# Hybrid attention block: gate projections of the 'b' heads turned token-major, transposes issued in pairs, key copies by DMA

## The chip, the cores and the metric

One core of a Trainium2 chip runs the whole layer. The metric is the device time of one execution in microseconds. Before the change it is 446.06 us, the median of three runs (445.18 to 448.8).

The engines are named as the profile names them: PE is TensorE (matmul), PEld its weight loads, DVE VectorE, ACT ScalarE, POOL GpSimd, SP SyncE, which here issues DMAs. A q behind a name (SPq) is that engine's instruction queue.

## The reference

```
h = x @ w_in                                  # x: 1024 tokens x 1024
q_a, k_a, v_a, z_a, q_b, k_b, v_b, z_b = split(h)
y_a = neighborhood_attention(q_a, k_a, v_a, rel_bias)      # 8 heads, 8x16 window on a 16x64 grid
y_b = windowed_gqa_with_sink(rotary(q_b), rotary(k_b), v_b, sink)   # 8 query heads, 2 key heads, |i-j| <= 128
mixed = concat(y_a * silu(z_a), y_b * silu(z_b))
y = mixed @ w_out
out = layer_norm(2**0.25 * x + y)
```

All products keep fp32-like precision: operands are split into a high and a low fp16 part, and high*high, high*low and low*high are added up.

## The kernel before

**Projections.** w_in is cut into 21 groups of 128 output columns, worked off in the list ORDER: q0 to q3, k0 to k3 and z0 to z3 for the 'a' heads, qb0 to qb3, kb and zb0 to zb3 for the 'b' heads (z is a gate; each group has two heads of 64). `project` (L358) does one group in two halves of 512 tokens, 24 matmuls of 512 columns for each half: the weight part is the stationary operand, x the moving one, and the result has the group's columns on the partitions and the tokens along the row. The weights' low and high parts are made by `w_split` (L191): ACT writes the high part (L199), POOL scales the raw weights and subtracts (L204, L205). The first six groups (NPRO) are done one after the other; the other 15 are filled in between the attention's matmuls, so many at each step (`pump_to`, FILL_AT).

**The attention.** 128 units: first 64 of the 'b' heads (group p, head j of the pair, block of 128 queries), then 64 of the 'a' heads. The main loop (L1181) has a step for each unit: `stage_qk` makes the scores in a PSUM bank (L816, L817; four banks) and DVE adds bias and takes the maximum (L826); `stage_exp` has ACT take the exponent (L842); one step later `stage_tr` splits the probabilities into high and low fp16 parts (ACT L852, DVE L853) and turns them by a DMA transpose from SP (L856). Four units are a quad. `stage_pv` multiplies the four units' turned probabilities with the values (L881, 33 or 36 matmuls of 64 columns), 9 steps after the quad's first unit; a step later `stage_on` divides by the sums (DVE L887, L890), giving `on` with the tokens on the partitions; after the quad of the pair's second head, `stage_ot` turns `on` by four PE transposes (L901), and DVE multiplies the result into the gate z (L904 for 'b', L910 for 'a').

**Queries and keys.** A block of a qb group is turned by rotary positions: ACT copies it from PSUM (L311), DVE shuffles it (L312), POOL multiplies by cos and sin and adds (L313 to L315). ACT then writes the high part for each of the two heads (L259) and POOL the low part (L265); the score matmul of the units that use them waits for that. For the keys, both parts are copied to the other 64 partitions by POOL (L295).

**The order of the work.** What is not written at its place goes through a recording layer: `enq` puts an operation in one of four queues (act, dve, pool, sp) with the operations it needs and a priority, and at fixed points of each step `pop` records the first one or two whose needs were recorded in an earlier step (for SP's results, two more steps later: `lag`). NP is the number that POOL gets at each step. `need` records an operation at once, with all that it needs, where a stage can't be recorded without it. What is recorded runs in that order on its engine.

**Output projection.** `m_queue` (L1009) splits the gated products m of the 'b' heads from step M_AT on: ACT high part (L1013), POOL low part (L1014). `out_mms` (L1021) multiplies 128 tokens of m with w_out; its first products fill the last steps, the rest follows after the attention (`final`), with the normalisation on DVE, ACT and POOL.

**Buffers.** z of each group has a tile of 1024 fp32; some share it with tables: the cos table has the slot "zc", which the gate zb3 gets later.

Of the kernel before, what the change touches and what calls it, by code (L numbers as in the profile page):

```python
# [15 lines left out]
S = 1024  # L16
# [20 lines left out]
ZTAG = {"z3": "zv", "zb3": "zc", "z2": "zs", "zb1": "zd", "zb2": "ze"}  # L37
# [9 lines left out]
WO_SCALE = 55  # L47
M_AT = [105, 112, 118, 120]
# [13 lines left out]
def hybrid_block(ctx, tc, xT, x, wt, wv, wo, bias, sink, gain, lbias, cos, sin, bmask, out):  # L62
# [220 lines left out]
    def split_k(p, half, src, dep=None):  # L283
# [3 lines left out]
        eng = "pool" if dep and clock["step"] is not None else "dve"  # L287
        for j in range(2):
            a, o = slice(64 * j, 64 * j + 64), slice(64 - 64 * j, 128 - 64 * j)
            hi, lo = split_hl(lambda j=j, a=a: own("kh", p, j)[a, sl], lambda j=j, a=a: own("kl", p, j)[a, sl],  # L290
                              src[a], dep is None, eng)

            def dup_(w, j=j, a=a, o=o):
                t = own(w, p, j)
                nc.gpsimd.tensor_copy(t[o, sl], t[a, sl])  # L295
# [4 lines left out]
            dup = [enq("pool", lambda d=dup_: d("kh"), o1, after=32 if dep else 0),  # L300
                   enq("pool", lambda d=dup_: d("kl"), o2, after=36 if dep else 0)]
            stk_ops.setdefault((p, j, half), []).extend(dup)
# [44 lines left out]
    def z_col(e):  # L347
        i = 0 if e in (4, 0, 5) else 1 if e == 1 else 2
# [8 lines left out]

    def project(name):  # L358
        n = ORDER.index(name)
# [397 lines left out]
    split = [ap.tile([128, 3, 2, 128], F16, name=f"split{i}", bufs=1) for i in range(NSPLIT)]  # L757
# [87 lines left out]
    def stage_tr(u):  # L845
        g, p, j, t, _ = u
        n, ch = geom(u)
        pt = st.pop((u, "p"))
        c, m = ch[0], len(ch)
        hl = split[units.index(u) % NSPLIT]  # L850
        src = pt[:, :n].rearrange("p (k c) -> p k c", c=c)
        nc.scalar.activation(hl[:, :m, 0, :c], src, AF.Copy, scale=PSCALE)  # L852
        nc.vector.scalar_tensor_tensor(hl[:, :m, 1, :c], src, PSCALE, hl[:, :m, 0, :c],  # L853
                                       op0=ALU.mult, op1=ALU.subtract)
        tr = ap.tile([128, 6, 128], F16, tag="tr", name="tr", bufs=BH)
        nc.sync.dma_start(tr[:, :2 * m, :], hl[:, :m].rearrange("p k i c -> p (k i c)"), transpose=True)  # L856
        st[u, "tr"] = tr
# [24 lines left out]

    def stage_on(q):
# [4 lines left out]
        if j == 0:  # L888
            on[g, p, h] = ap.tile([128, 4, 2, HD], F32, tag="on", name="on", bufs=2)
        nc.vector.tensor_mul(on[g, p, h][:, :, j, :], ps[:, :4 * HD].rearrange("p (m e) -> p m e", e=HD),  # L890
                             ri.unsqueeze(2).to_broadcast([128, 4, HD]))

    def stage_ot(q):
        g, p, j, h = quad(q)
        if j == 0:
            return
        need(*stk_ops.get(f"zb{p}" if g == "b" else f"z{p}", ()))
# [4 lines left out]
        if g == "b":  # L902
            z = zt[4 + p][:, 512 * h:512 * h + 512]
            nc.vector.scalar_tensor_tensor(z, ps, z_col(4 + p), z, op0=ALU.mult, op1=ALU.mult)  # L904
        else:
            for i in range(2):
                b = 2 * h + i
                z = zt[p].rearrange("p (r c) -> p r c", c=GW)[:, :, 16 * b:16 * b + 16]
                src = ps[:, 256 * i:256 * i + 256].rearrange("p (r c) -> p r c", c=16)
                nc.vector.scalar_tensor_tensor(z, src, z_col(p), z, op0=ALU.mult, op1=ALU.mult)  # L910
# [19 lines left out]
    def m_alloc(e):  # L930
        if e >= 4:
            t = big_tile(f"m{e}", (128, 2, S), F16)
        else:
            t = tiles["fp"].tile([128, 2, S], F16, tag="m", name=f"m{e}", bufs=4)
        mh[e], ml[e] = t[:, 0, :], t[:, 1, :]

    def m_split(e, sl, hi, lo):
        hi(mh[e][:, sl], zt[e][:, sl])
        lo(ml[e][:, sl], zt[e][:, sl], mh[e][:, sl])  # L939
# [69 lines left out]
    def m_queue(e):  # L1009
        m_alloc(e)  # L1010
        m_ops[e] = []
        for h in (slice(0, 512), slice(512, S)):
            o = enq("act", lambda h=h: nc.scalar.copy(mh[e][:, h], zt[e][:, h]))  # L1013
            m_ops[e].append(enq("pool", lambda h=h: nc.gpsimd.tensor_sub(  # L1014
                ml[e][:, h], zt[e][:, h], mh[e][:, h]), o))
# [5 lines left out]
    def out_mms(t, a, ps, es, c=(0, 512)):  # L1021
        o, w = c
        ts, cs = slice(128 * t, 128 * t + 128), slice(o, o + w)
        ps = ps[:, o:o + w]
        for e in es:
# [4 lines left out]
            for i, (lh, rh) in enumerate(((mh[e], woh), (mh[e], wol), (ml[e], woh))):  # L1030
                nc.tensor.matmul(ps, lh[:, ts], rh[:, cs],  # L1031
# [16 lines left out]
    def final():  # L1048
# [7 lines left out]
        for e in EO[4:]:  # L1056
            m_split(e, slice(0, 512), nc.scalar.copy, nc.vector.tensor_sub)
            for n in (WO_SEQ.index((e, 0)), WO_SEQ.index((e, 1))):
                wo_split(n)
        for e in EO[4:]:  # L1060
            m_split(e, slice(512, S), nc.scalar.copy, nc.vector.tensor_sub)
        gb, bb = gain_tile[0], zslot("bb")
# [113 lines left out]
    def gain_load():  # L1176
        gain_tile.append(zslot("gb"))
# [3 lines left out]
    for i in range(-LD, NU + LO):  # L1181
# [25 lines left out]
        if i == 131:  # L1207
            enq("sp", gain_load, *m_ops[4])
# [32 lines left out]
        pop("dve", ND if i < M_AT[1] else 2, same=True)  # L1241
        if i < NU:
            stage_exp(units[i])
        pop("act", NA if i < M_AT[0] and len(queues["act"]) < 5 else 2)
# [80 lines left out]
```

## Time and profile before

| what | us |
|---|---|
| median of 3 runs | 446.06 |
| the profiled execution | 446.49 |
| its span, first to last instruction | 444.7 |
| PE busy | 437.5 |
| DVE busy | 344.2 |
| ACT busy | 308.3 |
| POOL busy | 221.6 |

The TensorE clock was granted at 0.995 of full speed over the span. A page of the profile groups instructions: line, engine, operation, tile written and tiles read (out<-in), sizes (partitions x elements), how many; then the busy time, the mean time of one in ns, the idle time of the engine just before them and what ended most of it. A timeline has the start in us from the span's beginning, the length, the engine, the line and the operation; equal neighbours are merged (x2), and in square brackets stands the idle time before it and what ended it. The chain of waits is the work that ended last, followed back from the last instruction.

### The profile page before, as it was taken

What the parts mean: (1) busy time and instruction counts of PE and PEld (TensorE: products, weight loads), DVE (VectorE), ACT (ScalarE), POOL (GpSimd) and SP (SyncE); (2) the same over time, 40 slices, a digit from 0 to 9 for tenths busy, and PEclk for the clock granted to TensorE, in tenths of its full rate; (3) what the DMA queues carried; (4) which work ended last, traced back from release to release, by engine and by line L of the source; (5) the groups of instructions that cost most, each with busy time, mean ns of one, the idle gap of its engine ahead of it and who ended that gap; (6) DMA issues with size and microseconds to landing.
All of it is one profiled execution on the core that took longest, in us unless ns stands there. A gap on an engine that the chain in (4) does not pass through costs nothing.

```text
span 444.7 us, 9505 instructions
## 1 busy us (share of the span) xinstructions
PE 437.5 (98%) x3289; PEld 255.5 (57%) x3289; DVE 344.2 (77%) x849; ACT 308.3 (69%) x700; POOL 221.6 (50%) x235
## 2 busy tenths in 40 slices
PE   9999999999999999999999999999999999999994
PEld 8997754444445565655565655656555654444453
DVE  5978967438986898887988888888878837589944
ACT  5759789766499988887868887888778946302401
POOL 0110074646839558866506767765574405205740
PEclk9999999999999999999999999999999999999997
DMA  8921469984659999587978899998999998103612
GB/s 272 390 91 60 145 235 339 336 292 169 213 127 214 206 190 181 98 162 143 164 127 175 169 182 180 213 170 213 192 204 253 167 172 347 55 0 102 232 69 72
DMA packets 133841, 81.39 MB, mean 183 GB/s; under 512 B 101280, under 2 KB 113440, under 8 KB 133536
## 3 DMA queue, kind: packets, MB, share of 16 engines
q1 hardware_dynamic: 133648, 80.64, 75.4%
q8 instruction: 26, 0.43, 0.4%
q14 instruction: 23, 0.19, 0.2%
q10 hardware_dynamic: 144, 0.13, 0.1%
HBM read 50.34 MB, written 9.96 MB: 136 GB/s over the span
## 4 chain that ended last, share of the span: by engine, by line
PE 91%; DMA 3%; POOL 3%; DVE 1%; issue 1%; ACT 1%; SPq 0%; POOLq 0%; DVEq 0%; ACTq 0%
PE ps_pj L379 44%; PE ps_s L1031 9%; PE ps_s L486 6%; PE ps_t L881 6%; PE ps_pj L1031 5%; PE ps_t L1031 5%; PE ps_s L816 4%; PE ps_s L817 4%; PE ps_pj L486 3%; PE ps_t L486 3%; DMA bias<-in_bias 3%; PE ps_t L901 1%; POOL wl L205 1%; PE ps_t L412 1%; POOL ks L295 1%
## 5 line engine op out<-in xcount | busy, mean ns | idle before, releaser
L379 PE MATMUL ps_pj<-xf,wh 128*128 128x512 f16 x672 | 202.1, 379 | 0.1
L379 PE MATMUL ps_pj<-xf,wl 128*128 128x512 f16 x336 | 127.3, 379 | 0.0
L379 PEld LDWEIGHTS <-wh 128*128 128x128 f16 x672 | 63.7, 98 | 60.4 <-DVE ks L263 0.5
L842 ACT ACTIVATE ps_s<-sn,nm 128x385 f32<-128x385 f32 (+3 forms) x128 | 70.1, 548 | 25.1 <-DVE nm L826 24.6
L853 DVE SCALAR_TENSOR_TENSOR split<-ps_s,split 128x384 f16<-128x384 f32 (+2 forms) x128 | 65.7, 513 | 27.5 <-ACT split L852 25.9
L1031 PEld LDWEIGHTS <-m 128*128 128x128 f16 x432 | 40.0, 98 | 41.1 <-DVE m L939 0.2
L852 ACT ACTIVATE split<-ps_s 128x384 f16<-128x384 f32 (+2 forms) x128 | 57.8, 452 | 2.5 <-DMA tr<-split 0.2
L204 POOL TENSOR_SCALAR wr<-wr,wsc 128x512 f32<-128x512 f32 x26 | 20.6, 791 | 68.1 <-ACT wh L199 61.6
L379 PEld LDWEIGHTS <-wl 128*128 128x128 f16 x336 | 32.9, 98 | 37.4
L826 DVE CUSTOM_DVE_ANT_0 sn<-ps_s,bm,nsk 128x384 f32<-128x384 f32 (+1 forms) x64 | 40.7, 636 | 2.0 <-PE ps_s L817 1.7
L1031 PE MATMUL ps_s<-wo,m 128*128 128x512 f16 (+1 forms) x192 | 40.8, 366 | 0.0
L816 PE MATMUL ps_s<-ks,qs 128*128 128x384 f16 (+4 forms) x128 | 39.2, 306 | 0.3 <-DVE qs L263 0.3
L817 PE MATMUL ps_s<-ks,qs 128*128 128x384 f16 (+4 forms) x128 | 39.2, 306 | 0.0
L826 DVE CUSTOM_DVE_ANT_0 sn<-ps_s,bias,sg 128x264 f32<-128x264 f32 (+1 forms) x64 | 35.0, 547 | 4.5 <-issue 1.5
L881 PEld LDWEIGHTS <-tr 128*128 128x128 f16 (+1 forms) x1104 | 36.6, 98 | 2.2
L205 POOL TENSOR_TENSOR wl<-wr,wh 128x512 f16<-128x512 f32 x26 | 32.7, 1257 | 2.2
L788 POOL TENSOR_SCALAR bias<-bias,rsg 128x552 f32<-128x552 f32 (+1 forms) x24 | 19.1, 797 | 23.8 <-DMA bias<-in_bias 22.6
L295 POOL COPY ks<-ks 64x512 f16<-64x512 f16 x40 | 26.0, 661 | 7.1 <-DVE ks L263 2.8
L1086 ACT ACTIVATE sd<-mv,eps 128x1 f32<-128x1 f32 x8 | 2.4, 295 | 36.5 <-DVE mv L1084 35.2
L1031 PE MATMUL ps_pj<-wo,m 128*128 128x512 f16 (+1 forms) x144 | 26.2, 326 | 0.0
L1130 POOL TENSOR_TENSOR xr<-xr,gb 128x512 f32<-128x512 f32 x7 | 9.8, 1396 | 32.4 <-ACT xr L1127 32.4
L842 ACT ACTIVATION_READ_ACCUMULATOR ps_s<-sn,nm 128x1 f32 x128 | 24.4, 190 | 0.0
(188 smaller groups left out, 813.8 us busy)
## 6 DMA issues: line engine op xcount, KB each, us to landing
ws<-in_wt SPq DMA_DIRECT2D x15, 512.0 KB, 5.9
wr<-in_wt SPq DMA_DIRECT2D x26, 256.0 KB, 3.6
wor<-in_wo SPq DMA_DIRECT2D x22, 256.0 KB, 3.5
bias<-in_bias SPq DMA_DIRECT2D x16, 276.0 KB, 3.3
xr<-in_x SPq DMA_DIRECT2D x8, 512.0 KB, 9.6
out<-xr SPq DMA_DIRECT2D x15, 256.0 KB, 2.1
bias<-in_bias SPq DMA_DIRECT2D x8, 368.0 KB, 3.8
wvraw<-in_wv SPq DMA_DIRECT2D x9, 320.0 KB, 5.8
```

The lines of the kernel that those rows point to most:

```text
L205: nc.gpsimd.tensor_sub(l, raw, h)
L295: nc.gpsimd.tensor_copy(t[o, sl], t[a, sl])
L379: nc.tensor.matmul(ps, a[:, k % 4, :], mv, start=(k == 0 and i == 0), stop=(k == KT - 1 and i == 2))
L486: nc.tensor.matmul(ps[:, :320], lh[:, ts], rh[:, cs], start=(k == ko[0] and i == 0), stop=(k == ko[-1] and i == 2))
L816: nc.tensor.matmul(ps[:, :m], q, sl[0], start=True, stop=False)
L817: nc.tensor.matmul(ps[:, :m], q, sl[1], start=False, stop=True)
L826: nc.vector.tensor_tensor_reduce(sn[:, :m], ps[:, :m], bias_t, sg[:, c:c + 1], init, op0=ALU.add, op1=ALU.min, accum_out=nm)
L842: nc.scalar.activation(pt[:, :m], sn[:, :m], AF.Exp, bias=nm, scale=-1.0, accum_out=sm[:, k:k + 1])
L852: nc.scalar.activation(hl[:, :m, 0, :c], src, AF.Copy, scale=PSCALE)
L853: nc.vector.scalar_tensor_tensor(hl[:, :m, 1, :c], src, PSCALE, hl[:, :m, 0, :c], op0=ALU.mult, op1=ALU.subtract)
L881: nc.tensor.matmul(ps[:, HD * m:HD * m + HD], a, b_, start=(i == 0), stop=(i == len(mms) - 1))
L1031: nc.tensor.matmul(ps, lh[:, ts], rh[:, cs], start=(e == EO[0] and i == 0), stop=(e == EO[-1] and i == 2))
```

## The change

- The gate projections zb0 to zb3 are done token-major (`project_rows`): 128 tokens of x are the stationary operand, the weights the moving one, in 96 matmuls of 128 columns for each half; z then has the tokens on the partitions. All four come in the first six groups.
- `stage_on` of the 'b' heads multiplies by the gate's scale too, and POOL multiplies `on` into z. The four PE transposes and DVE's product of `stage_ot` are left out for the 'b' heads.
- As m of the 'b' heads now has the tokens on the partitions, `m_queue` puts its two fp16 parts side by side and turns them by two DMA transposes for each group, which write over z's tile. It runs from steps 26, 42, 57 and 80 instead of 105, 112, 118 and 120.
- The probabilities of two units share a buffer (3 buffers of two instead of 6 of one; 4 of two instead of 9 of one for the turned ones), and one DMA transpose turns both after the second.
- In the main loop the keys are copied to the other 64 partitions by DMA from SP instead of by POOL.
- An operation that needs a result of POOL is recorded one step later (`lag` 1 for pool).
- SP may record two operations at each step instead of one before step 118. z1 gets the slot of the cos table. The rows of gain and bias are loaded into other buffers. The scale of w_out is made at step 60 instead of 55.

```
-LTT, LPP, BP, BH, BR, ND, NA, NX, F1 = 1, 6, 2, 9, 5, 1, 1, 6, 0.2
-NSPLIT, NP = 6, 2
-ORDER = ["zb0", "z0", "zb1", "kb", "qb0", "z1", "qb1", "zb2", "qb2", "k0", "qb3", "zb3", "q0", "k1", "q1",
+LTT, LPP, BP, BH, BR, ND, NA, NX, F1 = 1, 6, 2, 4, 5, 1, 1, 6, 0.2
+NSPLIT, NP = 3, 2
+ORDER = ["zb0", "zb1", "zb2", "kb", "qb0", "zb3", "qb1", "z0", "qb2", "k0", "qb3", "z1", "q0", "k1", "q1",
          "k2", "q2", "z2", "k3", "q3", "z3"]
-ZTAG = {"z3": "zv", "zb3": "zc", "z2": "zs", "zb1": "zd", "zb2": "ze"}
+ZTAG = {"z3": "zv", "z1": "zc", "z2": "zs", "zb2": "zd", "z0": "ze"}
-WO_SCALE = 55
-M_AT = [105, 112, 118, 120]
+WO_SCALE = 60
+M_AT = [26, 42, 57, 80]
+POP2_AT = (105, 112)
...
-            self.prio, self.born, self.lag = prio, clock["step"], 2 if eng == "sp" else 0
+            self.prio, self.born, self.lag = prio, clock["step"], {"sp": 2, "pool": 1}.get(eng, 0)
...
             def dup_(w, j=j, a=a, o=o):
                 t = own(w, p, j)
-                nc.gpsimd.tensor_copy(t[o, sl], t[a, sl])
+                if live:
+                    nc.sync.dma_start(t[o, sl], t[a, sl])
+                else:
+                    nc.gpsimd.tensor_copy(t[o, sl], t[a, sl])
...
+    def project_rows(name):
...
+        for half in range(2):
+            ps = new_group()
+            need(w_ops[2 * n], w_ops[2 * n + 1])
+            for c in range(96):
+                t, k, i = c // 24, c // 3 % 8, c % 3
...
+                ts = slice(128 * t, 128 * t + 128)
+                h, l = parts[2 * n + k // 4]
+                a, b = ((x16h, h), (x16l, h), (x16h, l))[i]
+                nc.tensor.matmul(ps[:, ts], a[half, k][:, ts], b[:, k % 4, :], start=(c % 24 == 0), stop=(c % 24 == 23))
+                if c % 4 == 3 and c < 95:
+                    yield
+            groups.append(evac(name, half, ps))
+            yield
...
     def stage_tr(u):
...
+        o = 0 if i % 2 == first else 3
+        hl = split[i // 2 % NSPLIT]
...
-        tr = ap.tile([128, 6, 128], F16, tag="tr", name="tr", bufs=BH)
-        nc.sync.dma_start(tr[:, :2 * m, :], hl[:, :m].rearrange("p k i c -> p (k i c)"), transpose=True)
-        st[u, "tr"] = tr
+        if i % 2 == 0:
+            return
+        tr = ap.tile([128, 12, 128], F16, tag="tr", name="tr", bufs=BH)
+        w = 2 * (len(sizes[0][1]) + len(sizes[1][1]))
+        nc.sync.dma_start(tr[:, :w, :], hl.rearrange("p k i c -> p (k i c)")[:, :128 * w], transpose=True)
...
     def stage_on(q):
...
+        if g == "a":
+            nc.vector.tensor_mul(o, src, rb)
+            return
+        nc.vector.scalar_tensor_tensor(o, src, z_col(4 + p), rb, op0=ALU.mult, op1=ALU.mult)
+        z = zt[4 + p].rearrange("p (t j e) -> p t j e", j=2, e=HD)[:, 4 * h:4 * h + 4, j, :]
+        gate_ops.setdefault(4 + p, []).append(enq("pool", lambda: nc.gpsimd.tensor_mul(z, z, o), prio=0.6))
 
     def stage_ot(q):
         g, p, j, h = quad(q)
-        if j == 0:
+        if j == 0 or g == "b":
             return
...
     def m_queue(e):
...
+            o = enq("act", lambda hr=hr, z=z: nc.scalar.copy(hr[:, :, 0, :], z), *gate_ops[e])
+            o = enq("pool", lambda hr=hr, z=z: nc.gpsimd.tensor_sub(hr[:, :, 1, :], z, hr[:, :, 0, :]), o)
+            m_ops[e].append(enq("sp", lambda hr=hr, out16=out16: nc.sync.dma_start(
+                out16, hr.rearrange("p t i f -> p (t i f)"), transpose=True), o))
...
         if bulk["last"] != i or (queues["sp"] and i - queues["sp"][0].born > 2):
-            pop("sp", 1 if i < 118 else 3)
+            pop("sp", 2 if i < 118 else 3)
```

More of the change, by code (lines that the diff above doesn't have):

```diff
@@ L287, in split_k @@
         eng = "pool" if dep and clock["step"] is not None else "dve"
+        live = clock["step"] is not None
+        to = "sp" if live else "pool"
         for j in range(2):
@@ L756, in hybrid_block @@
     units = unit_list()
-    split = [ap.tile([128, 3, 2, 128], F16, name=f"split{i}", bufs=1) for i in range(NSPLIT)]
+    split = [ap.tile([128, 6, 2, 128], F16, name=f"split{i}", bufs=1) for i in range(NSPLIT)]
     sns = [ap.tile([128, 388], F32, name=f"sn{i}", bufs=1) for i in range(2)]
@@ L1056, in final @@
         for e in EO[4:]:
[L1057 removed]
+            m_split(e, slice(0, 4), nc.scalar.copy, nc.vector.tensor_sub)
             for n in (WO_SEQ.index((e, 0)), WO_SEQ.index((e, 1))):
```

89 lines of the change are left out of this document (53 added, 36 removed).

## The prediction

> **What bounds the kernel now.** I read the page first, then the chain of waits in order of time, then the timelines of single engines. The page gives the span, the busy time of TensorE (PE), and the shares of the chain that ended last:
>
> ```profile
> span 444.7 us, 9505 instructions
> ...
> PE 437.5 (98%) x3289; PEld 255.5 (57%) x3289; DVE 344.2 (77%) x849; ACT 308.3 (69%) x700; POOL 221.6 (50%) x235
> ...
> PE 91%; DMA 3%; POOL 3%; DVE 1%; issue 1%; ACT 1%; SPq 0%; POOLq 0%; DVEq 0%; ACTq 0%
> ```
>
> A busy PE need not be PE at its peak, so the pitch of its matmuls has to be seen. The chain (start, length, what) gives it, since there each matmul follows the one before:
>
> ```profile
> 68.72 10.38 PE ps_pj L379 x48
> ...
> 149.89 0.96 PE ps_t L881 x33
> ...
> 434.25 2.69 PE ps_pj L1031 x48
> ```
>
> So 48 matmuls of 512 columns take 10.38 us, 216 ns each; 64 columns take 29 ns, with a new 128x128 weight tile for each; 128 columns take 56 ns, again with new weights each. Hardly a gap stands between them: of the score matmuls of L816, which wait for the q and k copies, the groups by line show 0.3 us of idle time.
>
> ```profile
> L816 PE MATMUL ps_s<-ks,qs 128*128 128x384 f16 (+4 forms) x128 | 39.2, 306 | 0.3 <-DVE qs L263 0.3
> ```
>
> PE is fed without a break from the first projection to the last output product. What changes the time is therefore matmul time added or removed, and any wait that reaches PE. The profiled execution took 446.49 us for its span of 444.7, 1.8 us lie around the span, and it stands 0.4 above the median of 446.06. The sum is made against 446.49.
>
> **PE's own work.** The gate projections of the 'b' heads (zb0 to zb3) become token-major: each of 8 halves has 96 matmuls of 128 columns in place of 24 of 512. That is 768 x 56 = 43.0 us instead of 192 x 216 = 41.5, or +1.5. The transposes of L901 go for the 'b' heads, 32 of 64. Their price is the distance from four of them to the next matmul, in the PE timeline:
>
> ```profile
> 157.17 0.60 PE L901 MATMUL ps_t<-identf,on 128*128 128x128 f32 x4
> 157.61 1.13 PE L881 MATMUL ps_t<-vb,tr 128*128 128x64 f16 x33
> ```
>
> 0.44 us for four, so 8 x 0.44 = 3.5 us go. PE's work falls by 2.0 us. The first projection now wants both weight halves within 14 matmuls (0.8 us) where it wanted the second after 12 of 216 ns; GpSimd's (POOL's) second low part ended at 60.43, and PE began at 59.37:
>
> ```profile
> 59.27 1.16 POOL L205 TENSOR_TENSOR wl<-wr,wh 128x512 f16<-128x512 f32 x1
> ```
>
> 60.43 less 59.37 + 0.8 is 0.3 us late: +0.3.
>
> **What is put on GpSimd in the 'b' stretch.** Sixteen gate products of 128x256 (nearest row L1099, 0.73 us) = 11.7 us; six of the eight subtractions for the output's low parts (L1014's kind, 1.16 us) move there = 7.0 us; of the key copies that become DMAs only 8 lie here (0.66 us each) = -5.3.
>
> ```profile
> L1099 POOL TENSOR_TENSOR xr<-xr,gb 128x256 f32<-128x256 f32 x1 | 0.7, 728 | 0.2 <-DVE stats L1080 0.2
> ```
>
> ```profile
> L1014 POOL TENSOR_TENSOR m<-z,m 128x512 f16<-128x512 f32 x8 | 9.1, 1161 | 3.8 <-ACT m L1013 3.8
> L295 POOL COPY ks<-ks 64x512 f16<-64x512 f16 x40 | 26.0, 661 | 7.1 <-DVE ks L263 2.8 <-ACT ks L257 1.5 <-DMA wr<-in_wt 0.6
> ```
>
> The load alone would be carried. The place is what counts. GpSimd works in order, and two things of the change set its order: results of GpSimd are used a step later, which moves the last step of each 'b' query block (the subtraction of L265, for which the score matmul waits) back; and each gate product waits for VectorE's `on`, made at L890, with everything behind it in the queue waiting too. I followed the recording layer's rules through the built program. The first subtraction of a block was recorded at steps 26, 31, 42 and 48 for use at steps 32, 36, 48 and 52; it is now recorded at 30, 36, 44 and 51. The one at 36 is drawn out only by the score matmul that needs it. Ahead of it in GpSimd's queue stand the gates recorded at steps 30, 34 and 50. (Step n is the n-th score matmul, from 0.) The score matmuls of steps 30, 32, 34, 36, 50 and 52 in the PE timeline:
>
> ```profile
> 174.97 0.33 PE L816 MATMUL ps_s<-ks,qs 128*128 128x384 f16 x1
> ...
> 178.11 0.27 PE L816 MATMUL ps_s<-ks,qs 128*128 128x256 f16 x1
> ...
> 182.20 0.33 PE L816 MATMUL ps_s<-ks,qs 128*128 128x384 f16 x1
> ...
> 185.44 0.33 PE L816 MATMUL ps_s<-ks,qs 128*128 128x384 f16 x1
> ...
> 212.42 0.33 PE L816 MATMUL ps_s<-ks,qs 128*128 128x384 f16 x1
> ...
> 215.66 0.33 PE L816 MATMUL ps_s<-ks,qs 128*128 128x384 f16 x1
> ```
>
> VectorE's `on` of steps 30, 34, 42 and 50, and (last) of step 110, whose score matmul stands below it:
>
> ```profile
> 177.39 0.42 DVE L890 TENSOR_TENSOR on<-ps_t,ri 128x256 f32<-128x256 f32 x1
> 184.87 0.42 DVE L890 TENSOR_TENSOR on<-ps_t,ri 128x256 f32<-128x256 f32 x1
> 199.55 0.42 DVE L890 TENSOR_TENSOR on<-ps_t,ri 128x256 f32<-128x256 f32 x1
> 215.91 0.42 DVE L890 TENSOR_TENSOR on<-ps_t,ri 128x256 f32<-128x256 f32 x1
> ...
> 328.66 0.42 DVE L890 TENSOR_TENSOR on<-ps_t,ri 128x256 f32<-128x256 f32 x1
> ```
>
> ```profile
> 327.05 0.28 PE L816 MATMUL ps_s<-ks,qs 128*128 128x264 f16 x1
> ```
>
> So `on` ends 2.8, 3.1 and 3.9 us after the score matmul of its step at 30, 34 and 50, and 2.0 us where VectorE keeps up best. It was nothing's business, since the next use was PE's transposes three steps on. Now GpSimd's queue hangs on it. Its rows:
>
> ```profile
> 163.00 1.27 POOL L313 TENSOR_TENSOR rp_raw<-rp_raw,cos 128x512 f32<-128x512 f32 x1 [3.07 <-DVE rp_sw L312]
> ...
> 169.72 2.38 POOL L265 TENSOR_TENSOR qs<-rp_raw,qs 64x512 f16<-64x512 f32 x2
> ...
> 173.44 0.69 POOL L204 TENSOR_SCALAR wr<-wr,wsc 128x512 f32<-128x512 f32 x1
> 174.22 1.16 POOL L205 TENSOR_TENSOR wl<-wr,wh 128x512 f16<-128x512 f32 x1
> ...
> 179.14 1.15 POOL L265 TENSOR_TENSOR qs<-rp_raw,qs 64x512 f16<-64x512 f32 x1
> ...
> 204.57 1.27 POOL L313 TENSOR_TENSOR rp_raw<-rp_raw,cos 128x512 f32<-128x512 f32 x1
> ...
> 211.16 1.16 POOL L265 TENSOR_TENSOR qs<-rp_raw,qs 64x512 f16<-64x512 f32 x1 [2.75 <-ACT qs L259]
> ```
>
> Before, the subtractions ended 7.2, 5.2 and 3.3 us ahead of steps 32, 36 and 52 (178.11 - 170.88, 185.44 - 180.29, 215.66 - 212.32). Now, counted from the score matmul at the gate's step, with 0.08 us between dependent GpSimd instructions (173.44 + 0.69 to 174.22) and 0.05 for the gated `on`, a scalar_tensor_tensor (477 ns, L910) where a multiply took 424:
>
> ```profile
> L910 DVE SCALAR_TENSOR_TENSOR z<-ps_t,zc,z 128x256 f32<-128x256 f32 x16 | 7.0, 477 | 7.8 <-PE ps_t L901 7.8
> ```
>
> A, step 32: `on` 2.89, gate 0.81, subtraction 1.23: ready at 4.9, due at 178.11 - 174.97 = 3.1. Late by 1.8 (1.0 with the best `on`). The queue itself says the same: from 163.00 and one step of 1.6 later, two rope products 2.5, two weight splits 3.7, two gates 1.5, rope sum, product, product 3.8, two output subtractions 2.3, one query subtraction 1.2: 15.0 us, ending at 179.6 for 178.1.
>
> B, step 36: `on` 3.14, gate 0.81, a weight split 2.0 that stands between, subtraction 1.23: 7.2, due at 3.24. Late by 3.9; 2.9 if VectorE has caught up while PE stood at A. I take 3.2.
>
> C, steps 45 to 48: ScalarE (ACT) writes z1 over the cos table and so waits for GpSimd's last cos product. It did so before, for 1.75 us, with no loss on PE:
>
> ```profile
> 205.87 0.69 ACT L341 ACTIVATE z<-ps_pj,invt 128x512 f32<-128x512 f32 x1 [1.75 <-POOL rp_raw L313]
> ```
>
> Now ahead of that product stand a gate that waits for `on` at 199.97, two output subtractions, a split and two query subtractions: 199.97 + 0.8 + 2.3 + 2.0 + 1.2 + 1.2 + 1.3 = 208.8, 2.9 later than 204.57 + 1.27. The four score banks cover some of that; between 0 and 2.9 I take 1.0.
>
> D, step 52: `on` 3.96, gate 0.81, subtraction 1.23: 6.0, due at 3.24. Late by 2.8; 0.8 with the best `on`; I take 2.2.
>
> A to D: 8.2 us, from 4.7 to 11.4.
>
> **Transposes in pairs.** A DMA goes out after the second unit of a pair, with up to 12 blocks instead of 6.
>
> ```profile
> L856 SPq DMA_TRANSPOSE tr<-split x128: 1188/1212/2615, 126.1 to 361.3; - x128
> ...
> DMA to landing us min/median/max: 2.5/3.4/6.2
> ```
>
> The sync queue (SP) is freed of 64 issues of 1.2 us and gets 8 for the output parts and 32 key copies; it was not PE's bound, so no gain. The last unit of a quad has no time to give: its transpose went out with the pair of issues at 139.14, plus 3.4 is 142.5, and PE took it at 142.93.
>
> ```profile
> 139.14 2.50 SPq L856 DMA_TRANSPOSE tr<-split  x2
> ```
>
> ```profile
> 142.93 1.12 PE L881 MATMUL ps_t<-vb,tr 128*128 128x64 f16 x33
> ```
>
> A pair's landing is not in the trace: between 3.4 (size costs nothing) and 6.8 (all doubles). Issues hardly vary with size, so I stay near the low end: half a microsecond, felt by a few of 32 quads, +2.0 (0 to 16). The key copies are wanted at least 7 steps after they can start and cost nothing; uncovered, each would cost a landing of some 3 us. On SP a key copy waits for the ACT or VectorE part that it copies, with transposes behind it; these parts are recorded a step earlier, so I cost it at nothing. The buffers hold 6 units of split as before and 8 of tr; a buffer of split comes free one step later, 1.6 us of a cover of 6 steps less a landing. The output's parts are made some 40 steps ahead, and the gain and bias rows only change buffers. VectorE loses 8 x 0.75 us of L904-like products and is no bound; if it kept up better for it, A to D would go to their low ends.
>
> **Sum.** -2.0 + 0.3 + 8.2 + 2.0 = +8.5: 446.49 + 8.5 = 455.0.
>
> **Rivals.** N, not slower: VectorE, with less to do, brings `on` within 2.0 us, and C is covered. Then A to D cost 1.0 + 2.9 + 0 + 0.8 = 4.7, pairs nothing: 446.5 - 2.0 + 0.3 + 4.7 = 449.5; if also step 36 finds its block ready, the work alone is left, 444.8. For it: steps 74 to 110 show `on` as early as 2.0. Against: in the 'b' stretch it was 2.2 to 4.4. It decides once the waits together are under 6.1 us. P: pairs land 1 us after PE is ready in half of the quads: 455 + 14 = 469. For it: the margin of 0.4 above; against: VectorE and ACT catch up at each wait. L: the weight loads, not the columns, pace the token-major matmuls. A weight load's own length is 98 ns:
>
> ```profile
> L379 PEld LDWEIGHTS <-wh 128*128 128x128 f16 x672 | 63.7, 98 | 60.4 <-DVE ks L263 0.5
> ```
>
> 768 x (98 - 56) = 32 us more, 487. Against it are the 48 matmuls at 56 ns and the 33 at 29. The Trainium skill, TensorE: Matmul & The Clock Gate, section Back-to-back issue gap, speaks for L in part: it gives about 81 ns as the sustained distance of 128-column matmuls with a weight load each. By it the projections would cost 768 x 25 ns = 19 us more, an estimate, and the kernel 474; this trace's 56 ns, though over 48 only, disagrees.
>
> **Chances.** Mine (450.5 to 461) 0.63, N 0.27, P 0.07, L 0.03. The likeliest gives 455. The range of 8 in 10 runs from N's end to 462. About 1% of the time is what a measurement of this kernel can tell from no change: 441.6 to 450.5. Faster needs more than PE's work gives: 0.02. Same is the rest of N and a little of mine: 0.27. Slower 0.71.
>
> **What would show it.** PE's score matmuls waiting for GpSimd's subtraction at steps 32, 36 and 52, 2 to 4 us each, with a gate product or weight split just ahead on GpSimd; ACT's z waiting over 3 us for cos; 768 matmuls at 56 ns (10.8 us per gate projection); 32 transposes left. Wrong if the score matmuls wait for nothing (N), the products of L881 wait for DMA (P), or a gate projection takes 15 us or more (L).

## The result, and the profile after

The changed kernel takes 460.62 us, the median of six runs (459.99 to 463.94), against 445.91 for the kernel before in the same runs: a ratio of 1.033, interval 1.0289 to 1.0371. The profiled execution took 460.95 us for a span of 459.1, 14.5 more than the profiled one before. Its page, the lines that answer to those shown of before:

```profile
PE 438.9 (96%) x3833; PEld 276.5 (60%) x3833; DVE 343.1 (75%) x841; ACT 309.0 (67%) x700; POOL 213.3 (46%) x216
...
PE 82%; POOL 7%; DVE 3%; DMA 3%; issue 2%; ACT 2%; SPq 0%; POOLq 0%; DVEq 0%; ACTq 0%
...
L850 PE MATMUL ps_s<-ks,qs 128*128 128x384 f16 (+4 forms) x128 | 39.7, 310 | 11.5 <-POOL qs L266 9.5
```

PE is no longer the whole chain: GpSimd has 7% of it, and the score matmuls (now L850) stood 11.5 us where they stood 0.3. The waits of PE (us in total, times, longest):

```profile
PE ps_s L850 <- POOL qs L266: 9.5, 3, 3.5
...
PE ps_s L850 <- DVE split L890: 1.8, 1, 1.8
PE ps_t L922 <- DMA tr<-split: 1.7, 2, 0.9
```

Three waits for GpSimd's query subtraction (L266), one for a score bank, two for a paired transpose. A wait costs a little more than the profile's idle time, since matmuls overlap at their ends; in what follows it is the distance from one matmul's start to the next, less the usual distance of its shape. That gives 2.7 us at 178.4 (A, step 32), 3.7 at 190.1 (B, step 36), 1.9 at 217.3 (C), 3.6 at 225.1 (D, step 52), and 1.05 and 1.0 for the transposes at 268 and 301. A and what follows it, in the PE timeline:

```profile
178.41 0.38 PE L413 MATMUL ps_pj<-xf,wl 128*128 128x512 f16 x1
181.34 0.28 PE L850 MATMUL ps_s<-ks,qs 128*128 128x256 f16 x1 [2.55 <-POOL qs L266]
...
182.37 1.06 PE L413 MATMUL ps_pj<-xf,wh 128*128 128x512 f16 x2
183.22 0.63 PE L413 MATMUL ps_pj<-xf,wl 128*128 128x512 f16 x1
```

From 182.37 two matmuls take 0.85 us to the next one's start, where two take 0.43 elsewhere. These matmuls wait for nothing; they run at half speed. The same spell comes after D, and none after B. In the table of windows the granted clock says so (the column after POOL's); the windows are the stretches around A, B and D, each 3.41 us long, as long as a spell:

```profile
178.65:182.06 3.41, 0.86 (x6) 0.46 (x6) 3.15 (x9) 2.04 (x5) 3.05 (x4) 1.00 0.73 136
182.06:185.47 3.41, 3.41 (x29) 1.98 (x28) 1.60 (x7) 1.79 (x5) 1.71 (x2) 0.50 1.13 113
188.89:192.30 3.41, 1.60 (x8) 0.57 (x6) 2.33 (x5) 2.59 (x8) 2.55 (x3) 1.00 0.62 119
192.30:195.71 3.41, 1.68 (x9) 0.85 (x10) 1.14 (x3) 1.19 (x3) 2.70 (x3) 1.00 0.32 92
226.44:229.85 3.41, 0.94 (x5) 0.51 (x6) 2.70 (x7) 2.04 (x5) 2.98 (x4) 1.00 1.12 208
229.85:233.26 3.41, 3.41 (x33) 2.14 (x32) 1.91 (x6) 2.73 (x6) 2.35 (x3) 0.50 0.61 128
```

The two spells cost 3.1 us together. GpSimd's timeline shows what stands ahead of the subtractions of A, B and D:

```profile
176.86 2.27 POOL L1066 TENSOR_TENSOR hr<-z,hr 128x512 f16<-128x512 f32 x2
179.34 0.72 POOL L940 TENSOR_TENSOR z<-z,on 128x256 f32<-128x256 f32 x1 [0.21 <-DVE on L938]
180.14 2.38 POOL L266 TENSOR_TENSOR qs<-rp_raw,qs 64x512 f16<-64x512 f32 x2
...
189.46 0.72 POOL L940 TENSOR_TENSOR z<-z,on 128x256 f32<-128x256 f32 x1 [5.60 <-DVE on L938]
...
192.82 1.15 POOL L266 TENSOR_TENSOR qs<-rp_raw,qs 64x512 f16<-64x512 f32 x1 [0.74 <-ACT qs L260]
...
225.02 0.69 POOL L205 TENSOR_SCALAR ws<-ws,wsc 128x512 f32<-128x512 f32 x1 [1.59 <-ACT wh L200]
225.79 1.15 POOL L206 TENSOR_TENSOR wl<-ws,wh 128x512 f16<-128x512 f32 x1
226.91 0.72 POOL L940 TENSOR_TENSOR z<-z,on 128x256 f32<-128x256 f32 x1
227.71 1.15 POOL L266 TENSOR_TENSOR qs<-rp_raw,qs 64x512 f16<-64x512 f32 x1
```

At A GpSimd waited only 0.2 us for `on`: it was busy till then. At B it stood 5.6 us for `on`, but the subtraction then waited 0.74 more for ScalarE's high part of the same query block (L260), which was itself recorded only when the score matmul needed it. At D it waited for `on` not at all: a weight split, held 1.6 us by ScalarE, and the gate stand ahead. `on` itself, in VectorE's timeline, was hardly earlier at A and D; it ended at 179.26 and 226.50, where GpSimd came to the gate at 179.13 and 226.91:

```profile
178.77 0.48 DVE L938 SCALAR_TENSOR_TENSOR on<-ps_t,zc,ri 128x256 f32<-128x256 f32 x1
...
226.01 0.48 DVE L938 SCALAR_TENSOR_TENSOR on<-ps_t,zc,ri 128x256 f32<-128x256 f32 x1
```

C is the cos table; ScalarE's timeline:

```profile
216.97 0.69 ACT L347 ACTIVATE z<-ps_pj,invt 128x512 f32<-128x512 f32 x1 [3.59 <-POOL rp_raw L319]
```

The rest of the change, in the chain of waits and in the page of the transposes' line:

```profile
68.98 10.74 PE ps_pj L383 x192
```

```profile
L896 SPq DMA_TRANSPOSE tr<-split x64: 1252/1460/3021, 128.3 to 373.2; - x64
...
DMA to landing us min/median/max: 3.4/4.0/6.4
```

192 token-major matmuls take 10.74 us, 56 ns each, and a pair lands 0.6 us later than a single transpose did (median 4.0 against 3.4). The wait at 268 ended with the landing of the pair issued at 264.02. Its second unit's split had ended at 262.98 (VectorE, L890); the queue was busy with two key copies:

```profile
262.80 1.12 SPq L299 DMA_DIRECT2D ks<-ks  x2
264.02 2.12 SPq L896 DMA_TRANSPOSE tr<-split  x1
```

The pair that PE took at 301.60 had its data at 296.24 and was issued at 297.77, behind an output part and two key copies.

### The profile page after: what moved, and what is told of

Read it like the earlier page. It is cut to its first block, busy times and chain, and to the rows that moved or that the text cites. A ratio compares the mean times of both kernels' runs of the same rounds, so it can differ in the third digit from the quotient of the medians.

```text
span 459.1 us, 10361 instructions
## 1 busy us (share of the span) xinstructions
PE 438.9 (96%) x3833; PEld 276.5 (60%) x3833; DVE 343.1 (75%) x841; ACT 309.0 (67%) x700; POOL 213.3 (46%) x216
## 4 chain that ended last, share of the span: by engine, by line
PE 82%; POOL 7%; DVE 3%; DMA 3%; issue 2%; ACT 2%; SPq 0%; POOLq 0%; DVEq 0%; ACTq 0%
PE ps_pj L413 31%; PE ps_pj L383 9%; PE ps_s L1084 8%; PE ps_t L922 6%; PE ps_s L520 6%; PE ps_pj L1084 5%; PE ps_t L1084 5%; PE ps_s L850 3%; PE ps_s L851 3%; PE ps_pj L520 3%; PE ps_t L520 2%; DMA tr<-split 2%; POOL qs L266 1%; POOL wl L206 1%; DVE sn L860 1%
## 5 line engine op out<-in xcount | busy, mean ns | idle before, releaser
L413 PE MATMUL ps_pj<-xf,wh 128*128 128x512 f16 x544 | 164.9, 381 | 0.0
L413 PE MATMUL ps_pj<-xf,wl 128*128 128x512 f16 x272 | 103.9, 382 | 0.0
L890 DVE SCALAR_TENSOR_TENSOR split<-ps_s,split 128x384 f16<-128x384 f32 (+2 forms) x128 | 65.6, 513 | 25.4 <-ACT split L889 24.7
L413 PEld LDWEIGHTS <-wh 128*128 128x128 f16 x544 | 51.5, 98 | 45.5 <-issue 0.4
L860 DVE CUSTOM_DVE_ANT_0 sn<-ps_s,bm,nsk 128x384 f32<-128x384 f32 (+1 forms) x64 | 40.7, 637 | 15.0 <-PE ps_s L851 14.5
L850 PE MATMUL ps_s<-ks,qs 128*128 128x384 f16 (+4 forms) x128 | 39.7, 310 | 11.5 <-POOL qs L266 9.5
L413 PEld LDWEIGHTS <-wl 128*128 128x128 f16 x272 | 26.7, 98 | 30.3 <-issue 0.6
L383 PEld LDWEIGHTS <-xf 128*128 128x128 f16 x768 | 43.2, 98 | 0.6 <-issue 0.3
L383 PE MATMUL ps_pj<-wh,xf 128*128 128x128 f16 x512 | 43.4, 219 | 0.0
L383 PE MATMUL ps_pj<-wl,xf 128*128 128x128 f16 x256 | 43.2, 219 | 0.1
L1084 PEld LDWEIGHTS <-m 128*128 128x128 f16 x216 | 20.2, 98 | 21.4 <-DVE m L986 0.2
L1084 PEld LDWEIGHTS <-z 128*128 128x128 f16 x216 | 20.0, 98 | 19.7
L850 PEld LDWEIGHTS <-qs 128*128 128x128 f16 x128 | 12.6, 98 | 26.6 <-POOL qs L266 11.0
```

Of the source, the lines that this page charges most:

```text
L383: nc.tensor.matmul(ps[:, ts], a[half, k][:, ts], b[:, k % 4, :], start=(c % 24 == 0), stop=(c % 24 == 23))
L413: nc.tensor.matmul(ps, a[:, k % 4, :], mv, start=(k == 0 and i == 0), stop=(k == KT - 1 and i == 2))
L850: nc.tensor.matmul(ps[:, :m], q, sl[0], start=True, stop=False)
L860: nc.vector.tensor_tensor_reduce(sn[:, :m], ps[:, :m], bias_t, sg[:, c:c + 1], init, op0=ALU.add, op1=ALU.min, accum_out=nm)
L890: nc.vector.scalar_tensor_tensor(hl[:, o:o + m, 1, :c], src, PSCALE, hl[:, o:o + m, 0, :c], op0=ALU.mult, op1=ALU.subtract)
L1084: nc.tensor.matmul(ps, lh[:, t, :], rh[:, cs], start=(e == EO[0] and i == 0), stop=(e == EO[-1] and i == 2))
```

## The experiments

Two theories were held against each other first: LAG (results of GpSimd used a step later make the last subtraction of a query block late) and GATE (the gate product, waiting for `on`, holds it up); PAIRS stands for the transposes. After the first four runs they became GPSIMD (its order) and QUEUE (the sync queue). For all runs together, PE's loss between 58 and 430 us, by the measure above: waits of score matmuls, waits for transposes, the loss in stretches whose granted clock was 0.5 (half speed), and all (with small other waits), in us. The waits are of the one profiled execution of each kernel. The runs were made in sets, between which the median of the kernel before moved from 445.6 to 446.7, so medians of different sets can differ by 1 us for that alone (changed; e1 to e4; e5 to e8; e9 to e11; e12).

| kernel | median | ratio to before, interval | score | transposes | half speed | all |
|---|---|---|---|---|---|---|
| before | 446 | | 0.4 | 0 | 0 | 0.7 |
| changed | 460.6 | 1.033 (1.0289 to 1.0371) | 12.4 | 2.1 | 3.1 | 17.9 |
| e1: no lag | 457.4 | 1.0272 (1.0249 to 1.0296) | 3.8 | 7.2 | 1.4 | 13.1 |
| e2: before, lag alone | 456.9 | 1.0261 (1.0231 to 1.0292) | 8.8 | 0 | 2.9 | 11.7 |
| e3: gates on VectorE | 465.3 | 1.0439 (1.0416 to 1.0462) | 12.6 | 3.3 | 5.4 | 22.6 |
| e4: single transposes | 481.7 | 1.0792 (1.0727 to 1.0856) | 13.9 | 14.0 | 12.4 | 41.0 |
| e5: e1, output parts late | 460.7 | 1.0333 (1.0314 to 1.0352) | 6.7 | 8.0 | 0 | 17.1 |
| e6: e1, gates later | 456.7 | 1.0234 (1.0194 to 1.0275) | 1.7 | 8.8 | 0 | 11.4 |
| e7: e1, key copies on GpSimd | 453.8 | 1.0174 (1.0154 to 1.0194) | 6.7 | 2.1 | 0 | 10.2 |
| e8: e7, single transposes | 456.7 | 1.0228 (1.0188 to 1.0269) | 6.5 | 1.4 | 1.7 | 11.2 |
| e9: lag for other engines only | 450.8 | 1.0093 (1.0059 to 1.0127) | 3.3 | 2.9 | 0 | 7.2 |
| e10: e9, a cos product on VectorE | 450.1 | 1.0081 (1.0049 to 1.0114) | 0.4 | 6.0 | 0 | 6.9 |
| e11: e10, key copies on GpSimd | 449.1 | 1.0056 (1.0031 to 1.0082) | 0.8 | 2.8 | 1.5 | 5.6 |
| e12: e11, output parts moved | 448.3 | 1.0051 (1.0035 to 1.0068) | 1.8 | 1.2 | 0 | 4.8 |

**e1, the lag undone.**

```
-            self.prio, self.born, self.lag = prio, clock["step"], {"sp": 2, "pool": 1}.get(eng, 0)
+            self.prio, self.born, self.lag = prio, clock["step"], {"sp": 2}.get(eng, 0)
```

> The changed kernel with one thing undone: a result of GpSimd may be used in the step after the one it was recorded in, as before (the lag of 1 for GpSimd goes). The changed kernel took 460.6 us, with four waits of TensorE for the query copies and the score banks of 2.7, 3.7, 1.9 and 3.6 us (11.9) and two spells of matmuls at twice their time that follow two of them (about 3.1). Theory LAG (the step of lag is what makes the last low part of each 'b' query block late): all four waits and both spells go, 460.6 - 15 = 445.6, between 443 and 450. Theory GATE (the subtraction stands behind a gate product that waits for VectorE's 'on', whatever the lag): the waits at steps 32, 36 and 52 stay at two thirds or more, 455 to 460. Theory PAIRS (the time goes on the paired transposes): 459 to 461, no change.

457.4: neither. By its number it lies in GATE's range, but GATE's waits are gone: all waits for query subtractions went, C too, and the two spells with them, as LAG has it; but some 12 us came in other places, which no theory had. One chain of them is seen whole. GpSimd, then ScalarE, then PE:

```profile
143.32 0.73 POOL L940 TENSOR_TENSOR z<-z,on 128x256 f32<-128x256 f32 x1 [1.22 <-DVE on L938]
```

```profile
151.02 0.62 ACT L260 CAST qs<-rp_raw 64x512 f16<-64x512 f32 x1 [2.62 <-POOL rp_raw L321]
```

```profile
152.67 0.32 PE L850 MATMUL ps_s<-ks,qs 128*128 128x384 f16 x1 [1.60 <-DVE split L890]
```

The gate waits for `on`, the rope sum behind it comes late, ScalarE's cast, now recorded a step earlier, stands for the sum with the splits of the probabilities behind it, and the score banks come free late. So without the lag ScalarE pays for GpSimd's lateness, with it PE does. The transposes' 7.2 us come next.

**e2, the lag alone**, on the kernel before (the same line, the other way).

> The kernel before with one part of the change done alone: the lag of 1 for results of GpSimd. No token-major gates, no gate products on GpSimd, single transposes, key copies on GpSimd. Theory LAG: waits of TensorE at score steps 36 and 52 of 3 to 4 us each, perhaps 1 to 2 us at the score banks near step 48, and spells of slow matmuls behind them: 445.9 + 8 to 12 = 454 to 458. Theory GATE: without gates in GpSimd's queue the subtractions come in time, since before they ended 3.3 to 7.2 us ahead: 445.5 to 447.5. Theory PAIRS: no change, 446.

456.9, as LAG expects: 11.3 us for one line. The waits stand at steps 36, 49 (a score bank) and 52; at step 32 there is none, so A takes more than the lag. GATE's claim, that without gates there is no wait, is out:

```profile
PE ps_s L816 <- POOL qs L265: 7.0, 2, 4.0
```

**e3, the gate products on VectorE.**

```
-enq("pool", lambda: nc.gpsimd.tensor_mul(z, z, o), prio=0.6)
+enq("dve", lambda: nc.vector.tensor_mul(z, z, o), prio=0.6)
```

> The changed kernel with the sixteen gate products of the 'b' heads on VectorE instead of GpSimd; the lag, the pairs and the early output parts stay. Theory GATE: GpSimd no longer waits for 'on', the waits at steps 32, 36 and 52 (2.7 + 3.7 + 3.6 = 10.0) go with the slow spells behind them: 460.6 - 13 = 447.6, 446 to 451. Theory LAG: the subtractions are still recorded a step too late, the waits at 32 and 36 stay over 2 us each and the one at 52 at half or more: 456 to 461. Theory PAIRS: 459 to 461.

465.3, above what any theory gave. B stays to the tenth, 3.7 us, with no gate in GpSimd's queue; A grows to 4.2, and GpSimd's rope products ahead of it began at 168.87 instead of 165.50 (why was not tried). At step 52 the wait falls from 3.6 to 1.7, ended by a score bank within 0.1 us of the subtraction; in place of C, step 48 now waits 2.5 us for a subtraction. So A and B are late without any gate in GpSimd's queue, and the gate may have a part in D. What the gate adds in the changed kernel is not shown by this run, since here the queue itself ran later. B here:

```profile
196.31 0.50 PE L850 MATMUL ps_s<-ks,qs 128*128 128x384 f16 x1 [3.54 <-POOL qs L266]
```

**e4, single transposes**, with 6 buffers of one unit and 8 turned ones:

```
+        n, ch = geom(u)
+        c, m, o = ch[0], len(ch), 0
+        hl = split[i % NSPLIT]
...
+        tr = ap.tile([128, 6, 128], F16, tag="tr", name="tr", bufs=BH)
+        nc.sync.dma_start(tr[:, :2 * m, :], hl[:, :m].rearrange("p k i c -> p (k i c)"), transpose=True)
+        st[u, "tr"] = tr
```

> The changed kernel with each unit turned by its own DMA again (6 buffers of split, 8 of tr), everything else as changed. Theory LAG or GATE with the pairs priced at 2.0 us as forecast: the two waits of TensorE for a transpose at 268 and 300 us (1.05 and 1.0) go, 460.6 - 2.0 = 458.6, 457.5 to 460. Theory PAIRS (pairs carry the loss): 446 to 452. A third way: the sync queue, with 64 more issues of 1.2 us beside the 32 key copies, becomes late itself: 461 to 465, with waits of TensorE for the transposes at other places.

481.7, 17 us beyond the third way. The sync queue's timeline shows why: from 262 to 282 us it issues almost without a break, and between the transposes stand key copies, bias rows and an output part.

```profile
268.62 1.24 SPq L1060 DMA_TRANSPOSE z<-hr  x1
269.97 2.64 SPq L890 DMA_TRANSPOSE tr<-split  x2
272.66 0.58 SPq L818 DMA_DIRECT2D bias<-in_bias  x1
273.34 1.21 SPq L890 DMA_TRANSPOSE tr<-split  x1
274.61 1.23 SPq L299 DMA_DIRECT2D ks<-ks  x2
```

So the pairs save 21 us by the medians once the key copies and the output parts are on that queue. Not all of it is the queue: waits for transposes grew by 11.9 us, and of the 12.4 at half speed 8.0 follow A, B and D, which wait for GpSimd; there the changed kernel lost 3.1, by where the spells happened to fall (see the last section).

**e5 to e8** start from e1 and take one load away each. e5: `M_AT = [70, 80, 90, 100]`.

> The changed kernel without the lag (the run that took 457.4 us), and with the output's low and high parts of zb0 to zb3 made at steps 70, 80, 90 and 100 instead of 26, 42, 57 and 80: their subtractions on GpSimd (1.16 us each) and their 8 transposes on the sync queue (1.24 us each) leave the 'b' stretch. In the run without the lag TensorE waited 7.2 us for paired transposes (2.4 and 1.6 of it at 191 and 225 us, where a transpose of the output parts was issued shortly ahead), 3.4 us for score banks, and 1.3 us went on slow matmuls. Theory QUEUE (the sync queue has become the bound: key copies and output parts are issued ahead of the paired transposes): the waits at 191 and 225 go with the slow spell, 457.4 - 5.4 = 452, 450 to 454. Theory GPSIMD (GpSimd's order holds ScalarE, and with it the score banks): the 3.4 us of bank waits shrink, since 7 us leave GpSimd; at most 454, and the waits for transposes stay. If the paired transposes are slow in themselves: no change, 456 to 458.

460.7, above all that was expected. The waits at 191 and 225 went, as QUEUE says, but as many came in the 'a' stretch, where the parts now meet bias rows, values and key copies (2.3 us at 334, five of 0.8 to 1.1), and 2.5 us at a bank at 212: the load was moved, not lifted.

e6 records each gate product five steps after its `on`:

```
+        ready = Op("sp", None, [], 1)
+        ready.step = clock["step"] + 2
+        ... enq("pool", lambda: nc.gpsimd.tensor_mul(z, z, o), ready, prio=0.6)
```

> The changed kernel without the lag, and with each gate product recorded five steps after its 'on' instead of in the same step, so that GpSimd finds 'on' ready. In the run without the lag GpSimd stood 1.2 us for 'on' at 142 us, its rope sum came late, ScalarE stood 2.6 us for it, and TensorE 1.8 us for the score bank at 151 us. Theory GPSIMD: that wait of 1.8 us goes, and of the other bank waits (0.3, 0.8, 0.5) most: 457.4 - 3 = 454.4, 453 to 456. Theory QUEUE: the waits for transposes (7.2 us) and the slow spell stay at least as they were. Both together give 454; below 451 would say that the transposes too are late because of the gates.

456.7 (454.4 to 458.3), not to be told from e1's 457.4 (456.3 to 458.9). In the profile the bank wait at 151 went, as GPSIMD has it, which confirms e1's chain; the waits for transposes grew from 7.2 to 8.8, 3.7 of it at one place, and took much of the gain.

e7 puts the key copies back on GpSimd (`to = "pool"`, and the copy by `nc.gpsimd.tensor_copy`).

> The changed kernel without the lag, and with the 32 key copies back on GpSimd (40 copies of 0.66 us in all, as before) instead of DMAs on the sync queue; pairs, gates on GpSimd and early output parts stay. Theory QUEUE: the waits for transposes (2.4, 1.6, 0.5, 1.3, 1.2 = 7.2 us, most with two or three key copies issued just ahead of them) shrink to the two or so that an output part causes, and the slow spell goes: 457.4 - 5 to 6 = 452, 450 to 454. Theory GPSIMD: GpSimd gets 21 us more, 5.3 of them in the 'b' stretch, and its waits grow: 458 to 462.

453.8, as QUEUE expects: the waits for transposes fall to one of 2.1, though GpSimd has more to do. The bank waits grow by 2.9, as GPSIMD expects in kind but not in size:

```profile
PE ps_s L847 <- DVE split L887: 4.8, 4, 2.3
PE ps_t L919 <- DMA tr<-split: 2.0, 1, 2.0
```

e8 is e7 with the single transposes of e4.

> As the run with the key copies back on GpSimd and no lag, and with single transposes too: what is left of the change is the token-major gates with their product on GpSimd and the output parts made early. Theory QUEUE: the changed kernel with single transposes took 481.7 us because the sync queue had 32 key copies beside 128 issues of 1.2 us; without the copies single transposes cost little: within 3 us of the run with pairs and copies on GpSimd, 450 to 455. If instead single transposes are too dear beside anything on that queue: 460 to 480.

456.7, above QUEUE's 450 to 455 but at 2.9 us from e7 by medians, with runs from 453.7 to 457.9, so only this much is told: beside key copies on GpSimd single transposes cost some us or nothing, and not 21. That speaks for QUEUE. It is no clean pair with e4, which had the lag too; single transposes with key copies on the sync queue and no lag were not run.

**e9, the lag kept for other engines**, and dropped where GpSimd uses its own result:

```
-            d.step is not None and d.step + d.lag < clock["step"] + ...
+            d.step is not None and d.step + (0 if d.eng == eng == "pool" else d.lag) < clock["step"] + ...
```

> The changed kernel with the lag for results of GpSimd kept where another engine uses them, and taken away where GpSimd itself does (the rope sum after its two products, the gate-free chain of GpSimd); all else as changed. With the lag everywhere TensorE waits for the query low parts (460.6 us); with none, ScalarE stands 2.6 us for a rope sum at 148 us and holds the score banks, and paired transposes come late (457.4). Theory GPSIMD-ORDER (each of the two is a matter of one step, and the chain from the rope products to the subtraction pays the step twice): the waits at 32, 36 and 52 fall under 1 us each, the bank wait at 151 does not come back, the wait for the cos table stays at about 1: 460.6 - 10 - 3 = 447.6, 446 to 451. Theory QUEUE (once TensorE no longer stands for GpSimd, the paired transposes are late by themselves, 7 us as in the run with no lag): 452 to 456.

450.8, in the upper part of what GPSIMD-ORDER gives and under QUEUE's: 9.8 us from one line. The query block comes a step sooner, and ScalarE stands 0.6 us for the rope sum, once, where it stood 2.6 in e1. Left are C, 1.8, and two waits for transposes:

```profile
PE ps_t L922 <- DMA tr<-split: 2.6, 2, 1.5
PE ps_s L850 <- DVE split L890: 2.3, 3, 1.7
```

**e10, the last cos product on VectorE.**

```
+        last = live and half == 1 and name == "qb3"
+        o3 = enq("dve" if last else eng, lambda: (nc.vector if last else mul).tensor_mul(raw, raw, tiles["cos"][:, sl]), o2, after=3)
```

> As the run with the lag for other engines only, and the last cos product (qb3, second half, 128x512) on VectorE instead of GpSimd, so that ScalarE may write z1 over the cos table sooner. Where the wait C was 1.9 us with the lag everywhere and 2.4 without it, the theory that it is the cos table gives 1 to 2.4 us less than the run beside it: 446 to 449; the rival, that C comes from ScalarE or VectorE being late in themselves, gives no change (within 0.7) or a loss of 0.6, which is the product's time on VectorE.

450.1, 0.8 less, under the 1 to 2.4 expected, and with intervals that overlap. C is gone, so the cos table was its cause; but a wait of 2.4 us for a pair at 196 came in the same profile, so most of the gain was not kept.

**e11, e10 with the key copies on GpSimd** (e7's edit).

> As the run with the cos product on VectorE, and the 32 key copies back on GpSimd. Without any lag this took 3.6 us off (457.4 to 453.8), because the sync queue no longer had key copies ahead of the paired transposes. Theory QUEUE: waits for transposes of some us remain in the run beside it, and go here: 2 to 4 us less than it, 443 to 447, at or under the 446 of the kernel before, since TensorE has 2.0 us less to do. Theory GPSIMD-ORDER: GpSimd has room outside the 'b' stretch but not in it (5.3 us more there): the waits for the query low parts come back by 1 to 3 us, and the two cancel: within 1.5 of the run beside it.

449.1, 0.9 less, with intervals that overlap: above QUEUE's 443 to 447, and by its number what GPSIMD-ORDER gave (within 1.5), though the waits for query low parts that this theory expected did not come. The waits for transposes at 196 and 256 went and the one at 289 fell to 0.3 (QUEUE), and one of 2.4 at 218 came, with a spell behind it. The sync queue ahead of it:

```profile
211.92 3.13 SPq L1065 DMA_TRANSPOSE z<-hr  x2
215.09 0.58 SPq L996 DMA_DIRECT2D wor<-in_wo  x1
216.16 1.26 SPq L894 DMA_TRANSPOSE tr<-split  x1
```

**e12, e11 with the output parts of three groups moved**, `M_AT = [26, 57, 75, 95]`.

> As the run with lag for other engines only, the last cos product on VectorE and the key copies back on GpSimd (449.1 us), and the output parts of zb1, zb2 and zb3 made at steps 57, 75 and 95 instead of 42, 57 and 80. In that run one wait of some size is left that the kernel before did not have: 2.4 us at 218 us for a paired transpose that the sync queue issued 1.4 us after its data stood ready, behind two transposes of output parts and a weight load, with 1.2 us of slow matmuls after it. Theory QUEUE: it goes and nothing comes in its place, 449.1 - 0.4 - 2.4 - 1.2 = 445.1, 444 to 447, which is the time of the kernel before or up to 2 us under it. Rival: a pair is late at this place for its data and not for the queue, or the parts collide with loads of the 'a' stretch instead (as when all four were moved to steps 70 to 100): 448 to 452.

448.3, above QUEUE's 444 to 447, at the low edge of the rival's range. The wait at 218 went as QUEUE says, but not for nothing: a dozen waits of 0.2 to 0.6 us are left.

No version made here beats the kernel before. e12 comes nearest, and its sum closes: PE's work is 2.0 less, the waits are 4.8 - 0.7 = 4.1 more, and the time from the last matmul on is 0.7 less, together +1.4; the two profiled executions differ by 448.07 - 446.49 = 1.6.

## Why the prediction was right, and where it was not

The direction, the place of the waits and the range were right; the time was 5.6 us short. By its steps, against the profiled execution (+14.5):

- **PE's own work, -2.0.** Right. 768 token-major matmuls at 56 ns: 43.0 us. L fell with it, which wanted 98 ns, and 18.8 us for what took 10.74. The Trainium skill, TensorE: Matmul & The Clock Gate, section Back-to-back issue gap, gives about 81 ns for such a stream with a weight load each; here 768 of them kept 56 ns.
- **First projection, +0.3.** Right: 0.31 at 59.7.
- **A to D, +8.2.** Right in place, and the term that was mis-sized: 2.7, 3.7, 1.9 and 3.6 make 11.9, over its upper end of 11.4. A and D exceed their own upper ends (1.8 and 2.8). The prediction made the wait for `on` the start of A, B and D, 2.9, 3.1 and 4.0 us after the score matmuls of steps 30, 34 and 50. Here `on` ended 3.8, 2.3 and 4.4 us after them. At A and D GpSimd's queue came free within 0.4 us of `on`, so both held the subtraction, and at A both were later than counted (the prediction's own sum of the queue had it end at 179.6; it ended at 181.3). At B, ScalarE's part came last. e3 shows A and B without any gate, so the step that fails is `on` as the cause: it was one of several chains that were late together. That B's 3.7 lies near the 3.2 taken is luck. The prediction named the lag beside the gate, and the lag is the larger: alone it costs 11.3 (e2), though none of it at A. C came by the mechanism named (e10), at 1.9 for 1.0.
- **Half speed after a wait: not in the sum**, +3.1. No row of before could show it, since PE never stood so long there between 58 and 430 us.
- **Pairs, +2.0.** Right in its number, 2.06, and by luck. The extra landing was 0.6 where half a microsecond was taken, but not a few quads felt it: both waits stand behind key copies on the sync queue, which were costed at nothing, and with the copies back on GpSimd (e7) the waits at these two places are gone, with pairs as before.
- **What was costed at nothing.** Key copies and output parts on the sync queue were not free: beside the pairs, the copies cost 3.6 us without the lag (e1 against e7). The prediction said that the queue was freed and that this gained nothing; without the freed issues the same load made the kernel 21 us slower (e4). The sentence named the cover, but not its price.
- The time from the last matmul to the end fell by 0.4.

The sum as measured: -2.0 + 0.3 + 11.9 + 3.1 + 2.1 - 0.4 = 15.0; 0.5 of it over the 14.5 is not explained. The miss of the prediction is 3.7 from A to D and 3.1 from half speed. Rival N fell: `on` came 2.3 to 4.4 us after the score matmuls, not within 2.0. P fell: two waits of 1 us, not half of the quads.

The theory that stands: in the 'b' stretch GpSimd, the sync queue and ScalarE each have so little slack that a delay put on one comes out on PE by another way. Undoing single parts (e1, e3 to e6) moved most of the loss or added to it. What lowered it was taking the doubled lag out of GpSimd's own chain (e9, 9.8 us), and load off the sync queue: 3.6 us without the lag (e7), 0.9 behind e9 and e10, which is inside the noise (e11). What stays open is whether the last 4.1 us of small waits can be had back, and what the new order of the projections and the second operation of SP at each step do alone; neither was tried. Nor is it settled why e8's runs spread.

## What to carry to other kernels

Where PE is fed without a break, a change that saves it 2 us is worth that only if no helper's order gets worse: look for the one result in each stage that PE needs last, and count the steps of every hop on its way, because a rule such as "use it a step later" is paid once for each hop. A rule that spares one engine a wait can be kept for that engine and dropped where the result stays on the engine that made it, whose operations ran in the recorded order in all these timelines. And when parts of a change share a queue, cost each without the others: the piece that looks neutral may be what carries the rest.

## What the runs showed of the hardware

The half-speed spells. Over all runs 14 of the 20 waits of PE of 2.4 us or more were followed by one, at a granted clock of 0.5; no single shorter wait was, and one spell (e4, 367 us) came after five waits of 0.4 to 1.0 us within 11 us.

The clock's record in the traces shows what decides. A spell lasts 3.41 us, or 6.83 (after five of the waits in e3 and e4), and within a run all spells begin on one beat of 3.41 us: those of the changed kernel begin at 182.06 and 229.85, 14 beats apart. Cut every run into its beats, and add up for each how long PE stood in it (distances from start to start over the usual ones). All 15 spells follow a beat at full clock in which PE stood 2.02 us or more, and no beat at full clock with less (1.97 at most) was followed by one. The windows shown above are such beats: A's 2.7 us fell into one; of D's 3.6, 2.5 fell into one; B's 3.7 were cut by a beat's end into 2.0 and 1.7, and went free. A spell of one beat cost 1.3 to 1.7 us, one of two beats up to 2.8. So whether a wait between 2.0 and 4 us is punished is chance here: it depends on where the beat falls.

The Trainium skill, TensorE: Matmul & The Clock Gate, sections What's actually happening and HAM oscillation — how this bites in real kernels, has the clock halved after an idle window of about 3.4 us that runs freely, and warns of idle gaps longer than that. The free-running window agrees with the beats here; the limit does not, since 2.44 us were enough in e1 and 3.67 not in e6.

Transposes from SBUF to SBUF: up to 12 blocks by one DMA instead of up to 6 cost the issue 1.46 us instead of 1.21 (medians of the changed kernel and the one before) and land 0.6 us later, so on a full queue a pair saves nearly a whole issue.
